# More modulation chunks on VectorE, shifted priorities, one-copy bank eviction, a new product order and a last norm with TensorE, in an encoder layer

## The chip, the cores and the metric

One core of a Trainium2 chip runs the whole kernel. The metric is the device time of one execution in microseconds (us), the median of several runs; lower is better. The engines are TensorE (PE in the profile; its weight loads have a row of their own, PEld), VectorE (DVE), ScalarE (ACT), GpSimd (POOL) and SyncE (SP), which issues most of the loads.

## The reference

One layer, 256 tokens of width 2048, fp32: attention and then an MLP, each with its own modulation from a vector c.

```python
# for each sub-layer:
h = x * (1 + scale(c)) + shift(c)
x = LayerNorm(alpha * x + (1 + gate(c)) * sublayer(h))
# attention: proj = h @ w_qkv + b_qkv, 32 query heads and 8 key/value heads of 64, rotary positions,
#   |q - k| <= 128, softmax with a learned sink per head, then o @ w_o + b_o
# MLP: relu(h @ w1 + b1)**2 @ w2 + b2, hidden width 8192
# LayerNorm: (x - mean) * rsqrt(var + 1e-5) * g + b over the 2048 columns
```

scale, shift and gate are matrix-vector products of the activated c with six matrices of 2048 x 2048.

## The kernel before

**Loads.** One stream (class `Stream`) holds a list of 1 MB loads, [128, 2048] fp32, planned once and issued in that order on SP's queue, as buffers (`raws`) come free. A load is either a part of a weight matrix, or a *modulation chunk*: two (for `m_gm`, one) groups of 128 rows of a modulation matrix. A group of matrices' columns (`Mod`) has 4 to 16 chunks; there are 80 of them beside the 16 of `m_gf`. `W1_FILL`, `SLOT_FILL` and `gf_fill` say how many late chunks stand between which weight loads.

**Modulation.** `Mod.step` uses a chunk in one of two ways. On TensorE, `quad` (L340) multiplies it in 32-column weight tiles with c and adds up in PSUM (8 instructions, 16 records of the trace each chunk). On VectorE, for the chunks whose number is in the tuple `dve`, it is multiplied by c's column, L376 (first) or L378 (added to the part so far), two of them for each chunk, and at the group's end one `quad` with ones sums over partitions. Then `columns` turns the row and `modulated(g)` (L565 to L567) scales and shifts x into a high part on ScalarE and a low part on VectorE.

**Weights.** Products of fp32 quality are made of three fp32r matmuls (`mm3`, L544 to L546): ScalarE rounds a load to its high part (`wh`, the cast L277), VectorE subtracts for the low part (`wl`, L230, *lows*). `Stream.pump` writes casts, lows and chunks into the program ahead of the matmuls that need them. Within an engine, the scheduler of the tile framework puts instructions in an order by priority (program order, if nothing shifts it) and readiness; on the chip each engine runs its list in that order.

**Stages.** qkv projection (to about 160 us) with the modulation groups 0 to 5; attention in 21 slots, where projection, rotary tables, scores, softmax, probabilities and the output projection are interleaved (to 355 us); the norm; the first block of W1 (L1032 to L1034); feed-forward blocks 1 to 3; the last columns of w2; the last norm.

**Feed-forward.** A block has 16 hidden tiles in 8 pairs. `hidden(f)` (L1060, L1062: 5.55 us) fills one PSUM bank with 256 columns of product and 256 of its correction, and `square_half` adds them and the bias, takes relu and square, and splits the result. `sides` makes sums of a pair's blocks (`sc`) for a scheme with 7 products instead of 8, and `chunk(i)` issues these 7 (21 matmuls) in two pieces around the second tile of the next pair:

```python
        for i in range(NP):
            g = chunk(i)
            if i + 1 < NP:
                hidden(2 * i + 2)
            next(g)
            if i + 1 < NP:
                hidden(2 * i + 3)
            for _ in g:
                pass
```

The products stay in seven PSUM banks over the whole block, so that one bank of the pool `psa` is left for the hidden tiles, and each must be read before the next tile starts.

**Tail.** For each half of the tokens (t = 0, 1), the last 512 columns of the output are multiplied, `add_gated` (L797 to L799) adds them to x and takes statistics, and the norm is written in four column blocks: L1217 (minus mean, times g) and L1222 (times rstd, plus b), one block of four with ScalarE (L1219) and GpSimd (L1220) instead.

## Time and profile before

| | |
|---|---|
| median of 3 runs | 1081.54 us (1081.45 to 1083.96) |
| the profiled execution | 1080.82 us, span 1079.0 us, mean TensorE clock 0.995 |
| instructions in the trace | 15651 |
| TensorE / its weight loads, busy | 97% / 79% |
| VectorE / ScalarE / GpSimd, busy | 86% / 57% / 3% |
| read from HBM | 289.57 MB |

The busy shares are means over the stages. Where TensorE is busy without a gap, a shorter wait elsewhere gives nothing; where it waits, the wait's last releaser counts. In rows of a timeline, the first number is the start, the second the duration, and the bracket the idle time before the row with what ended it.

### The profile page before, as it was taken

What the parts mean: (1) busy time and instruction counts of PE and PEld (TensorE: products, weight loads), DVE (VectorE), ACT (ScalarE), POOL (GpSimd) and SP (SyncE); (2) the same over time, 40 slices, a digit from 0 to 9 for tenths busy, and PEclk for the clock granted to TensorE, in tenths of its full rate; (3) what the DMA queues carried; (4) which work ended last, traced back from release to release, by engine and by line L of the source; (5) the groups of instructions that cost most, each with busy time, mean ns of one, the idle gap of its engine ahead of it and who ended that gap; (6) DMA issues with size and microseconds to landing.
All of it is one profiled execution on the core that took longest, in us unless ns stands there. A gap on an engine that the chain in (4) does not pass through costs nothing.

```text
span 1079.0 us, 15651 instructions
## 1 busy us (share of the span) xinstructions
PE 1049.8 (97%) x6018; PEld 847.9 (79%) x6018; DVE 926.3 (86%) x1371; ACT 611.4 (57%) x977; POOL 31.0 (3%) x56
## 2 busy tenths in 40 slices
PE   8889999999999999999999999999999999999995
PEld 6557677666667799988888888888888888888884
DVE  5598699988889898988679889969988887998997
ACT  5333347776773636644357677347767536776740
POOL 1000000001000000000000000000000001000001
PEclk9999999999999999999999999999999999999998
DMA  9999997779966798689725644954464684455632
GB/s 384 425 426 426 426 419 268 283 281 378 405 251 234 305 356 314 257 335 405 271 97 196 233 176 153 375 195 176 176 234 174 266 319 148 176 205 220 244 161 78
DMA packets 43371, 292.70 MB, mean 271 GB/s; under 512 B 5136, under 2 KB 5264, under 8 KB 9504
## 3 DMA queue, kind: packets, MB, share of 16 engines
q1 hardware_dynamic: 39312, 279.85, 66.7%
q0 software_dynamic: 3232, 10.50, 3.0%
q10 hardware_dynamic: 752, 1.35, 0.3%
q8 instruction: 47, 0.77, 0.3%
q14 instruction: 28, 0.23, 0.1%
HBM read 289.57 MB, written 2.11 MB: 270 GB/s over the span
## 4 chain that ended last, share of the span: by engine, by line
PE 85%; DMA 9%; DVE 4%; ACT 1%; issue 0%; SPq 0%; DVEq 0%; ACTq 0%
PE pa L1060 17%; PE pa L544 13%; PE pa L546 13%; PE pa L545 13%; PE pa L1062 8%; DMA raw<-in_wqkv 4%; PE pa L1033 3%; PE pa L1034 3%; PE pa L1032 3%; DMA raw<-in_modm 3%; PE pm L340 2%; DMA raw<-in_modf 2%; PE pa L733 1%; PE pa L789 1%; DVE wl L230 1%; DVE g L378 1%
## 5 line engine op out<-in xcount | busy, mean ns | idle before, releaser
L277 ACT CAST wh<-raw 128x1024 fp32r<-128x1024 f32 (+1 forms) x332 | 335.5, 1020 | 302.3 <-PE pa L546 136.2
L230 DVE TENSOR_TENSOR wl<-raw,wh 128x1024 fp32r<-128x1024 f32 (+1 forms) x332 | 388.5, 1183 | 79.8 <-ACT wh L277 74.6
L544 PE MATMUL pa<-wh,g 128*128 128x512 f32 x648 | 258.0, 399 | 4.4 <-ACT g L581 2.1
L546 PE MATMUL pa<-wh,g 128*128 128x512 f32 x648 | 252.2, 392 | 3.0 <-DVE g L567 2.4
L545 PE MATMUL pa<-wl,g 128*128 128x512 f32 x648 | 254.0, 392 | 0.0
L1060 PE MATMUL pa<-g,wh 128*128 128x512 f32 x768 | 193.4, 394 | 0.0
L1060 PEld LDWEIGHTS pa<-g,wh 128*128 128x128 f32 x768 | 139.8, 188 | 31.6 <-DVE rl L990 4.1
L544 PEld LDWEIGHTS pa<-wh,g 128*128 128x128 f32 x648 | 121.6, 188 | 39.3 <-issue 6.8
L546 PEld LDWEIGHTS pa<-wh,g 128*128 128x128 f32 x648 | 121.6, 188 | 33.1 <-DVE g L567 4.7
L545 PEld LDWEIGHTS pa<-wl,g 128*128 128x128 f32 x648 | 121.8, 188 | 25.9 <-issue 2.4
L1062 PEld LDWEIGHTS pa<-g,wl 128*128 128x128 f32 x768 | 104.8, 190 | 7.5
L1062 PE MATMUL pa<-g,wl 128*128 128x256 f32 x768 | 107.1, 283 | 0.0
L378 DVE SCALAR_TENSOR_TENSOR g<-raw,cact,g 128x1024 f32<-128x1024 f32 x65 | 82.6, 1278 | 1.5 <-DMA raw<-in_modf 1.3
L1033 PE MATMUL pa<-g,wh 128*128 128x256 f32 x256 | 72.7, 285 | 0.4 <-DVE g L961 0.4
L1032 PE MATMUL pa<-g,wh 128*128 128x256 f32 x256 | 72.6, 285 | 0.0
L1034 PE MATMUL pa<-g,wl 128*128 128x256 f32 x256 | 72.5, 284 | 0.0
L230 DVE TENSOR_TENSOR raw<-raw 128x1024 fp32r<-128x1024 f32 x48 | 58.7, 1223 | 8.5 <-ACT raw L277 6.6
L277 ACT CAST raw<-raw 128x1024 fp32r<-128x1024 f32 x48 | 50.6, 1054 | 12.0 <-PE pm L546 10.7
L340 PE MATMUL pm<-raw,cact 128*32 128x256 f32 (+2 forms) x768 | 47.3, 375 | 5.6 <-DMA raw<-in_modm 4.5
L1033 PEld LDWEIGHTS pa<-g,wh 128*128 128x128 f32 x256 | 49.1, 192 | 1.3 <-DVE g L961 0.8
L1032 PEld LDWEIGHTS pa<-g,wh 128*128 128x128 f32 x256 | 49.0, 192 | 0.4 <-ACT g L953 0.4
L1034 PEld LDWEIGHTS pa<-g,wl 128*128 128x128 f32 x256 | 49.1, 192 | 0.0
(220 smaller groups left out, 1210.0 us busy)
## 6 DMA issues: line engine op xcount, KB each, us to landing
raw<-in_w1b SPq DMA_DIRECT2D x48, 1024.0 KB, 5.6
raw<-in_w SPq DMA_DIRECT2D x40, 1024.0 KB, 8.4
raw<-in_modm SPq DMA_DIRECT2D x32, 1024.0 KB, 16.0
raw<-in_modf SPq DMA_DIRECT2D x32, 1024.0 KB, 8.8
raw<-in_wqkv SPq DMA_DIRECT2D x24, 1024.0 KB, 11.8
raw<-in_w2s SPq DMA_DIRECT2D x24, 1024.0 KB, 4.8
raw<-in_modgm SPq DMA_DIRECT2D x16, 1024.0 KB, 8.4
raw<-in_wo SPq DMA_DIRECT2D x16, 1024.0 KB, 7.6
```

What stands on the lines that cost most here:

```text
L230: self.pinned(nc.vector.tensor_sub(l[:, :w], r, f32(self.hs[n])[:, :w]))
L277: self.pinned(nc.scalar.copy(h[:, :s.shape[-1]], s))
L340: i = nc.tensor.matmul(self.ps[32 * j:32 * j + 32, :w], lhsT[j] if type(lhsT) is list else lhsT, rhs[j], start=self.first, stop=stop)
L378: nc.vector.scalar_tensor_tensor(p[:, :e], s, cact[:, kt:kt + 1], p[:, :e], op0=OP.mult, op1=OP.add)
L544: nc.tensor.matmul(ps, xh, wh, start=start, stop=False)
L545: nc.tensor.matmul(ps, xh, wl, start=False, stop=False)
L546: S.prev = nc.tensor.matmul(ps, xl, wh, start=False, stop=stop).ins
L1032: nc.tensor.matmul(o, wh(w, 128), hh, start=new, stop=False)
L1033: nc.tensor.matmul(o, wh(w, 128), hl, start=False, stop=False)
L1034: nc.tensor.matmul(o, wl(w, 128), hh, start=False, stop=end)
L1060: nc.tensor.matmul(ps, wh(k, 128), ff_in(k), start=k == 0, stop=False)
L1062: nc.tensor.matmul(ps[:, :256], wl(k, 128), ff_in(k)[:, :256], start=False, stop=k == NK - 1)
```

## The change

- **Chunks.** 40 chunks on VectorE instead of 36 (beside `m_gf`'s 16, unchanged), with other numbers in the tuples: one more in the fifth and one in the sixth group of the first modulation, one more in the second and one in the third group of the feed-forward's.
- **Load order.** New fill tables with the same totals. The first 56 loads on SP stay as they are; after these, chunks stand up to three places sooner or later between the weight loads.
- **Priorities.** `first(name)` wraps kinds of work in a priority shift, for the six names in `AHEAD` (evictions of partial sums, the sums of VectorE over w2's blocks, rotary products, the copies of transposed pairs and of probabilities, and `square_half`). Names that aren't in it are unchanged; `FREE = 9` leaves the pins of `modulated` as they were.
- **Bank.** `square_half` copies the hidden tile's whole bank with ScalarE, adds the halves in SBUF, and the bias goes into the relu.
- **Product order.** `chunk` yields after five of the seven products, and after two in the last two pairs of a block.
- **Tail.** For t = 0 all four column blocks are VectorE's. For t = 1, three of four blocks are scaled by g ahead of the statistics; TensorE adds b (a product with the identity) and -(mean/2)·q·g (one with a diagonal of it) in PSUM, and VectorE combines. `last_scalars` has fewer steps.

The fill tables and tuples as the diff has them:

```diff
+AHEAD = {'evict': -10, 'sums': -100, 'rope': 10, 'pairs': -10, 'probs': -100, 'square': -30}
+FREE = 9
...
+    def first(name):
+        n = AHEAD.get((stage[0], name), AHEAD.get(name))
+        return tc.high_priority(n) if n else nullcontext()
...
-    m_mix = groups(a["modm"], MIXG, [(), (), (), (0, 1, 4, 5), (1, 2, 4, 6, 7), (4, 7)])
-    m_ff = groups(a["modf"], FFG, [(0, 3, 7), (0, 1, 2, 4, 7), (3,), (0, 1, 2, 3, 4, 5, 6, 7)])
-    m_gm = Mod([a["modgm"][i] for i in range(NK)], 512, (3, 4, 5, 6, 9, 11, 12, 14), a["modgmb"])
+    m_mix = groups(a["modm"], MIXG, [(), (), (), (0, 1, 3, 6), (0, 2, 4, 5, 6, 7), (3, 5, 6)])
+    m_ff = groups(a["modf"], FFG, [(0, 3, 7), (0, 1, 3, 4, 5, 7), (3, 4), (0, 1, 2, 3, 4, 5, 6, 7)])
+    m_gm = Mod([a["modgm"][i] for i in range(NK)], 512, (3, 4, 5, 7, 9, 10, 12, 14), a["modgmb"])
...
-    SLOT_FILL = dict(enumerate([1, 1, 0, 1, 2, 2, 1, 1, 1, 3, 0, 3, 1, 5, 0, 4, 1, 4, 0, 2, 0, 0, 1], -2))
+    SLOT_FILL = dict(enumerate([0, 0, 3, 1, 2, 0, 0, 3, 0, 5, 1, 4, 1, 3, 0, 3, 2, 2, 0, 3, 0, 0, 1], -2))
...
     def square_half(ps, ft, u, uf, at):
 
         v = sml.tile([128, 512], F32, name="rl", tag="t2", bufs=4)
-        nc.scalar.activation(v[:, 256:], ps[:, 256:], AF.Identity, bias=b1[:, ft:ft + 1])
-        nc.vector.tensor_add(v[:, :256], v[:, 256:], ps[:, :256])
-        nc.scalar.activation(v[:, 256:], v[:, :256], AF.Relu)
...
+        with first("bank"):
+            nc.scalar.copy(v, ps)
+        with first("square"):
+            nc.vector.tensor_add(v[:, :256], v[:, :256], v[:, 256:])
+            nc.scalar.activation(v[:, 256:], v[:, :256], AF.Relu, bias=b1[:, ft:ft + 1])
...
             u = us[i]
+            at = 5 if i < NP - 2 else 2
+            for n, (p, x, c, r, e) in enumerate(((1, u, 0, 0, 0), (2, u, 2, 1, 1), (3, sc, 3, 1, 0),
+                                                 (5, sc, 0, 2, 0), (7, sc, 2, 2, 1))):
+                if n == at:
+                    yield
+                product(p, i, x, c, h[r], l[r], e)
+                if n in (0, 2, 4):
+                    S.done()
+            if at == 5:
+                yield
...
+        if t == 0:
+            add_gated(ps, t, 3, g2, st)
+            mv, rstd = norm_scalars(st[t])
+            for c in (1, 0, 2, 3):
+                z, (g, b) = part(xs, t, c), affine(c)
+                nc.vector.scalar_tensor_tensor(z, z, mv[:, 0:1], g, op0=OP.subtract, op1=OP.mult)
                 nc.vector.scalar_tensor_tensor(z, z, rstd, b, op0=OP.mult, op1=OP.add)
...
+            for c in range(3):
+                scaled(1, c)
+    pw = {}
+    for c in (1, 2, 3):
+        pw[c] = psa.tile([128, 512], F32, name="pa")
+        g, b = affine(c)
+        tc.keep_in_program_order(nc.tensor.matmul(pw[c], ident, b, start=True, stop=False))
+    with tc.high_priority(200):
+        add_gated(ps, 1, 3, g2, st)
+        rstd, nm = last_scalars(st[1])
+        dg = sml.tile([128, 128], F32, name="dg", tag="t2", bufs=4)
+        nc.scalar.activation(dg, ident, AF.Copy, scale=nm)
+    scaled(1, 3)
+    g, b = affine(0)
+    w = sml.tile([128, 512], F32, name="w", tag="t2", bufs=4)
+    nc.vector.scalar_tensor_tensor(w, g, nm, b, op0=OP.mult, op1=OP.add)
+    for c in range(4):
+        z, (g, b) = part(xs, 1, c), affine(c)
+        if c:
+            nc.tensor.matmul(pw[c], dg, g, start=False, stop=True)
+        nc.vector.scalar_tensor_tensor(z, z, rstd, pw[c] if c else w, op0=OP.mult, op1=OP.add)
+        store(1, c, z)
```

(`scaled(t, c)` multiplies a block by -g/2, `store` issues its write to HBM.) Line numbers of the changed kernel are 9 to 83 higher for the same work: L230 is L239, L376 and L378 are L389 and L391, L566 and L567 are L582 and L583, L1060 and L1062 are L1095 and L1097, L277 is L288, L544 to L546 are L558 to L560, and L797 to L799 are L826 to L828. Three places show how instructions move.

VectorE around the modulation of x for the fifth group (x in g4_595, its scales in scm; wl are lows, and g4_1092 or g4_1050 is VectorE's part of the sixth group's modulation). Before:

```order
L417 TENSOR_SCALAR scm_113<-scm_113 128x4
L230 TENSOR_TENSOR wl_1090<-raw_935,wh_1066 128x1024
L230 TENSOR_TENSOR wl_1161<-raw_935,wh_1088 128x1024
L376 TENSOR_SCALAR g4_1092<-raw_953,cact_110 128x1024
L566 TENSOR_SCALAR g4_595<-g4_595,scm_113,shm_114 128x256
L378 SCALAR_TENSOR_TENSOR g4_1092<-raw_953,cact_110,g4_1092 128x1024
L567 TENSOR_TENSOR g4_1114<-g4_595,g4_1113 128x256
L566 TENSOR_SCALAR g4_595<-g4_595,scm_113,shm_114 128x256
L567 TENSOR_TENSOR g4_1114<-g4_595,g4_1113 128x256
```

After:

```order
L431 TENSOR_SCALAR scm_113<-scm_113 128x4
L389 TENSOR_SCALAR g4_1050<-raw_899,cact_110 128x1024
L391 SCALAR_TENSOR_TENSOR g4_1050<-raw_899,cact_110,g4_1050 128x1024
L239 TENSOR_TENSOR wl_1079<-raw_929,wh_1055 128x1024
L239 TENSOR_TENSOR wl_1149<-raw_929,wh_1077 128x1024
L582 TENSOR_SCALAR g4_595<-g4_595,scm_113,shm_114 128x256
L583 TENSOR_TENSOR g4_1102<-g4_595,g4_1101 128x256
```

The chunk of the sixth group's modulation (L376 and L378, now L389 and L391) has moved from between the two lows and L567 to a place ahead of the lows.

PE in a feed-forward block, from a hidden tile's last correction (L1062, now L1097) to the next tile's first product; pa, pt and pm are PSUM banks, sc, g4 and raw the hidden values and the weights. Before, the shorter of the two gaps of a pair:

```order
L1062 MATMUL pa_5685<-g4_4137,wl_5643 128x256 x2
L544 MATMUL pt_5428<-wh_5641,g4_5533 128x512
L545 MATMUL pt_5428<-wl_5662,g4_5533 128x512
L546 MATMUL pt_5428<-wh_5641,g4_5533 128x512
L544 MATMUL pa_5429<-wh_5660,g4_5533 128x512
L545 MATMUL pa_5429<-wl_5673,g4_5533 128x512
L546 MATMUL pa_5429<-wh_5660,g4_5533 128x512
L544 MATMUL pa_5430<-wh_5660,sc_5675 128x512
L545 MATMUL pa_5430<-wl_5673,sc_5675 128x512
L546 MATMUL pa_5430<-wh_5660,sc_5675 128x512
L544 MATMUL pt_5431<-raw_5671,sc_5675 128x512
L1060 MATMUL pa_5754<-g4_3396,wh_5723 128x512 x2
```

After, the shorter gap:

```order
L1097 MATMUL pa_5586<-g4_4112,wl_5572 128x256 x2
L1097 MATMUL pa_5586<-g4_4113,wl_5572 128x256 x2
L558 MATMUL pa_5405<-raw_5526,sc_5497 128x512
L559 MATMUL pa_5405<-raw_5526,sc_5497 128x512
L560 MATMUL pa_5405<-raw_5526,sc_5497 128x512
L558 MATMUL pa_5406<-raw_5526,g4_5350 128x512
L559 MATMUL pa_5406<-raw_5526,g4_5350 128x512
L560 MATMUL pa_5406<-raw_5526,g4_5350 128x512
L1095 MATMUL pa_5657<-g4_3372,wh_5570 128x512 x2
```

The gap between two hidden tiles had 10 matmuls here and 11 at the other tile of the pair; now it has 6 here and 15 there.

ScalarE around the eviction of a hidden tile (pa to rl) in such a pair. Before:

```order
L277 CAST wh_5738<-raw_5602 128x1024
L1008 CAST sc_5675<-sf_5676 128x512
L277 CAST wh_5748<-raw_5645 128x1024
L989 ACTIVATE rl_5728<-pa_5685,pack_87 128x256
L277 CAST wh_5771<-raw_5645 128x1024
L277 CAST wh_5791<-raw_5726 128x512
L991 ACTIVATE rl_5728<-rl_5728 128x256
```

After:

```order
L288 CAST wh_5625<-raw_5548 128x1024
L288 CAST raw_5643<-raw_5548 128x1024
L288 CAST wh_5695<-raw_5574 128x1024
L1022 COPY rl_5629<-pa_5586 128x512
L1025 ACTIVATE rl_5629<-rl_5629,pack_87 128x256
L1027 ACTIVATE uf_5506<-rl_5629 128x256
L288 CAST raw_5676<-raw_5548 128x1024
L1029 CAST g4_5505<-uf_5506 128x256
```

The bank copy L1022 takes the place of L989; relu L1025 and square L1027 follow it with no cast between, and there is again a cast of the next weights ahead of the copy.

VectorE in the tail. Before, from `add_gated` of t = 1 on:

```order
L797 TENSOR_TENSOR tmp<-pa,g4b 128x512
L798 TENSOR_TENSOR g_2474<-g_2474,tmp 128x512
L799 BN_STATS st_9555<-g_2474 128x6
L803 BN_AGGR mv<-st_9555 128x2
L805 TENSOR_SCALAR ve<-mv 128x1
L1217 SCALAR_TENSOR_TENSOR g_2470<-g_2470,mv,g_9546 128x512
L809 RECIPROCAL r_9876<-sd 128x1
L1217 SCALAR_TENSOR_TENSOR g_2468<-g_2468,mv,g_9546 128x512
L811 SCALAR_TENSOR_TENSOR qq<-r_9876,ve 128x1
L1217 SCALAR_TENSOR_TENSOR g_2472<-g_2472,mv,g_9547 128x512
L812 TENSOR_SCALAR qq<-qq 128x1
L1217 SCALAR_TENSOR_TENSOR g_2474<-g_2474,mv,g_9547 128x512
```

After, first what stands ahead of t = 0's chain:

```order
L239 TENSOR_TENSOR g_9701<-raw,g_9699 128x1024
L239 TENSOR_TENSOR g_9705<-raw,g_9703 128x1024
L239 TENSOR_TENSOR g4b<-raw,g4b 128x1024 x2
L1271 SCALAR_TENSOR_TENSOR g_2466<-g_2466,g_9522 128x512
L1271 SCALAR_TENSOR_TENSOR g_2468<-g_2468,g_9522 128x512
L1271 SCALAR_TENSOR_TENSOR g_2470<-g_2470,g_9523 128x512
L826 TENSOR_TENSOR tmp<-pa,g4b 128x512
L827 TENSOR_TENSOR g_2472<-g_2472,tmp 128x512
L828 BN_STATS st_9530<-g_2472 128x6
L832 BN_AGGR mv<-st_9530 128x2
```

Then, from `add_gated` of t = 1 on:

```order
L826 TENSOR_TENSOR tmp<-pa,g4b 128x512
L827 TENSOR_TENSOR g_2472<-g_2472,tmp 128x512
L828 BN_STATS st_9531<-g_2472 128x6
L1248 BN_AGGR mv<-st_9531 128x2
L1271 SCALAR_TENSOR_TENSOR g_2472<-g_2472,g_9523 128x512
L1252 TENSOR_SCALAR ve<-mv 128x1
L1254 RECIPROCAL r_9860<-sd 128x1
L1256 SCALAR_TENSOR_TENSOR qq<-r_9860,ve 128x1
L1257 SCALAR_TENSOR_TENSOR qq<-qq,r_9860 128x1
L1259 SCALAR_TENSOR_TENSOR nmr<-mv,qq 128x1
L1300 SCALAR_TENSOR_TENSOR w<-g_9522,nmr,g_9524 128x512
L1305 SCALAR_TENSOR_TENSOR g_2466<-g_2466,qq,w 128x512
```

Three of the four scalings by g (L1271) have moved ahead of t = 0's `add_gated`; of t = 1's norm, one is left behind the aggregate, and the last four steps read PSUM or w.

More of the change, by code (lines that the diff above doesn't have):

```diff
@@ L229, in low @@
                 l = (g4, g4b)[kept - 1](F32R) if kept > 0 else wlp.tile([128, 1024], F32R, name="wl")
-            self.pinned(nc.vector.tensor_sub(l[:, :w], r, f32(self.hs[n])[:, :w]))
+            with first("low"):
+                self.pinned(nc.vector.tensor_sub(l[:, :w], r, f32(self.hs[n])[:, :w]))
             self.ls.append(l)
@@ L276, in pump @@
                     s = raw[:, j * 1024:j * 1024 + 1024]
-                self.pinned(nc.scalar.copy(h[:, :s.shape[-1]], s))
+                with first("cast"):
+                    self.pinned(nc.scalar.copy(h[:, :s.shape[-1]], s))
                 self.hs.append(h)
@@ L564, in modulated @@
             xt, sc, sh = xts.pop(k0 + k), scm[:, k0 + k:k0 + k + 1], shm[:, k0 + k:k0 + k + 1]
[L565 to L567 removed]
+            with first("modulated"):
+                keep(nc.scalar.activation(hh[:, s], xt, AF.Identity, scale=sc, bias=sh))
+                keep(nc.vector.tensor_scalar(xt, xt, sc, sh, op0=OP.mult, op1=OP.add))
+                keep(nc.vector.tensor_sub(hl[:, s], xt, f32(hh[:, s])))
         held[g] = hh, hl
@@ L579, in evict @@
             if new:
-                bq(pss[t], c)
-                nc.scalar.copy(av, pss[t])
-            else:
-                nc.vector.tensor_add(av, av, pss[t])
+                with first("evict0"):
+                    bq(pss[t], c)
+                    nc.scalar.copy(av, pss[t])
+            else:
+                with first("evict"):
+                    nc.vector.tensor_add(av, av, pss[t])
     def banks():
@@ L713, in pairs_T @@
                     nc.tensor.transpose(pt[:, i * 256 + t * 128:i * 256 + t * 128 + 128], src[:, x:x + 128], ident)
-            nc.scalar.copy(out[:, pr * 512:pr * 512 + 512], pt)
+            with first("pairs"):
+                nc.scalar.copy(out[:, pr * 512:pr * 512 + 512], pt)
         return out
@@ L742, in scores @@
[L742 to L750 removed]
+                with first("scores"):
+                    nc.tensor.matmul(pss[s][:, i], qT[j][p, x:x + 128], kT[p, j * 256:j * 256 + 256],
+                                     start=True, stop=True)
@@ L879, in hybrid_kernel @@
     S.behind = True
+    stage[0] = "attention"
     for n in range(21):
@@ L935, in hybrid_kernel @@
     S.behind = False
+    stage[0] = "feed"
     ff_columns(0)
```

249 lines of the change are left out of this document (132 added, 117 removed).

## The prediction

> **What bounds the kernel now.** I read the page first: engine shares, slices, chain.
>
> ```profile
> span 1079.0 us, 15651 instructions
> PE 1049.8 (97%) x6018; PEld 847.9 (79%) x6018; DVE 926.3 (86%) x1371; ACT 611.4 (57%) x977; POOL 31.0 (3%) x56
> PEclk9999999999999999999999999999999999999998
> DMA  9999997779966798689725644954464684455632
> PE 85%; DMA 9%; DVE 4%; ACT 1%; issue 0%; SPq 0%; DVEq 0%; ACTq 0%
> ```
>
> TensorE (PE) is busy for 97% of the span at full clock and holds 85% of the chain. So the time can change in three ways only: work taken off PE, the some 29 us in which PE isn't busy, and the end after its last matmul. The waits view says what PE waited for in the middle:
>
> ```profile
> PEld pa L1060 <- DVE rl L990: 4.1, 11, 0.4
> PE pa L546 <- DVE g L567: 2.4, 2, 1.7
> PE pm L340 <- DMA raw<-in_modf: 1.1, 1, 1.1
> PE pm L340 <- DVE g L378: 0.8, 1, 0.8
> PE pa L546 <- DVE g L792: 0.6, 1, 0.6
> ```
>
> These five are 9.0 us. The other side of the change is VectorE (DVE), which gets more to do. Its load by stage, from the windows view (columns: window, length, busy PE, PEld, DVE, ACT, POOL, clock, DMA share, GB/s):
>
> ```profile
> 100.00:150.00 50.00, 48.28 (x298) 34.04 (x297) 37.88 (x56) 19.64 (x25) 1.90 (x2) 1.00 1.01 426
> 150.00:200.00 50.00, 50.00 (x262) 36.36 (x261) 48.76 (x89) 32.08 (x74) 0.48 (x1) 1.00 0.75 286
> 250.00:300.00 50.00, 48.61 (x321) 32.00 (x321) 41.23 (x88) 32.30 (x82) 3.40 (x5) 1.00 1.00 406
> 350.00:400.00 50.00, 48.49 (x417) 43.35 (x416) 45.26 (x78) 28.26 (x40) 0.00 (x0) 1.00 0.85 318
> ```
>
> VectorE has 12 us free of 50 in the projection, but only 1 to 9 in the windows after it. DMA is full in the projection (1.01) and again at 250 to 300 us.
>
> **A. The projection: −2.2 us.** One stall is worth a close look, the 1.7 of the second wait row:
>
> ```profile
> 112.56 3.66 PE L340 MATMUL pm<-raw,cact 128*32 128x256 f32 x64
> 114.14 2.36 DVE L230 TENSOR_TENSOR wl<-raw,wh 128x1024 fp32r<-128x1024 f32 x2 [3.44 <-ACT wh L277]
> 116.42 0.74 DVE L376 TENSOR_SCALAR g<-raw,cact 128x1024 f32<-128x1024 f32 x1
> 116.95 0.40 PE L545 MATMUL pa<-wl,g 128*128 128x512 f32 x1
> 117.41 1.28 DVE L378 SCALAR_TENSOR_TENSOR g<-raw,cact,g 128x1024 f32<-128x1024 f32 x1
> 118.60 0.41 DVE L567 TENSOR_TENSOR g<-g,g 128x256 fp32r<-128x256 f32 x1
> 119.07 0.50 PE L546 MATMUL pa<-wh,g 128*128 128x512 f32 x1 [1.72 <-DVE g L567]
> ```
>
> A modulation chunk (L376 and L378, 2.02 us) stands on VectorE between the lows L230 and the L567 that PE waits for. Before those lows VectorE had been idle for 3.44 us. In the changed order the chunk stands ahead of the lows, so its 2.02 us fall into that idle time, and L567 can end right after the lows. PE would go on some 0.23 us after the L545 at 116.95, which saves 1.7 to 1.8 us. The load it reads is an earlier one than that of the lows, so it should have landed; if not, the lows wait behind it, and the 2 us are lost again.
>
> Two chunks more leave PE in this stage. One costs 3.66/4 = 0.92 us of PE (64 matmul records are four chunks), and 2.0 to 2.6 us of VectorE. The one of the fifth group lies where PE waits for loads anyway (DMA share 1.01): nothing. The one of the sixth counts 0.9. I give 0.5 back, for the modulated inputs of the sixth group come later behind the extra chunk, and SP's loads in this stage can't go faster than 426 GB/s. Sum −1.8 − 0.9 + 0.5 = −2.2; ends −3 and 0.
>
> **B. Norm and first feed-forward stage: −1.4 us.**
>
> ```profile
> 353.78 1.22 DVE L230 TENSOR_TENSOR wl<-raw,wh 128x1024 fp32r<-128x1024 f32 x1
> 354.54 0.39 PE L546 MATMUL pa<-wh,g 128*128 128x512 f32 x1
> 355.51 0.68 DVE L797 TENSOR_TENSOR tmp<-pa,g4b 128x512 f32<-128x512 f32 x1
> 360.83 0.44 PE L947 MATMUL pt<-ident,g 128*128 128x128 f32 x2
> ```
>
> After the last matmul of the attention output (ended 354.93) the chain to the next stage runs over VectorE; its first step L797 came 0.58 us late, behind L230. In the new order that low stands behind it: −0.5. PE fills this stretch with modulation chunks, so the chunk that the second feed-forward group hands to VectorE saves nothing here. The one of the third group lies among W1's products, where PE is the limit: −0.9. Ends −2 and +0.5 (VectorE is 45.26 of 50 there).
>
> **C. Attention: 0, from −2 to +4.** Four chunks are about 10 us more for VectorE in all, at most half of them in its busy windows. The three short stalls that PE has there by the waits rows (1.1, 0.8, 0.6) can go with the smoother spread of loads, and others can come: a chunk half of 1.28 us that stands ahead of what PE needs costs up to that each. Three of those would be 4 us. The priorities shift evictions, rope sums and copies by a few places; no row prices that alone. I take nothing.
>
> **D. Feed-forward: −3.0 us.** In each pair of hidden tiles PE waits for a bank:
>
> ```profile
> 612.44 1.04 ACT L277 CAST wh<-raw 128x1024 fp32r<-128x1024 f32 x1
> 613.39 0.47 ACT L989 ACTIVATE rl<-pa,pack 128x256 f32<-128x256 f32 x1
> 613.52 1.22 DVE L230 TENSOR_TENSOR wl<-raw,wh 128x1024 fp32r<-128x1024 f32 x1 [0.26 <-ACT wh L277]
> 614.66 0.41 DVE L990 TENSOR_TENSOR rl<-rl,pa 128x256 f32<-128x256 f32 x1
> 614.79 0.39 PE L544 MATMUL pt<-raw,sc 128*128 128x512 f32 x1
> 615.13 2.14 PE L1060 MATMUL pa<-g,wh 128*128 128x512 f32 x8
> 1024.31 0.59 ACT L1117 COPY w<-pa 128x512 f32<-128x512 f32 x1
> ```
>
> The bank is read twice, by ScalarE (L989) and then by VectorE (L990), and L990 stood behind a low of 1.22 us. It ended at 615.07, and PE took the bank at 615.13, 0.11 later than its pace allowed for PE itself and 0.37 for its weight load. Now ScalarE copies the whole bank; the copy of that size in L1117 took 0.59, and VectorE's queue no longer counts. The new order of the products leaves 15 matmuls after the first tile of a pair (15 × 0.227 = 3.4 us), but only 6 after the second (1.36 us; before, 10 and 11). A cast of 1.04 us stands ahead of the copy. If it begins 0.8 us before the tile ends, as its wh buffer comes free, it ends 0.25 after it, the copy at 0.84, and with 0.06 for the hand-over PE has the bank at 0.90, 0.46 before it needs it. So the stalls go: 4.1 us. But the weight load overlaps PE, so I count three quarters: −3.0. In the chain that turns a tile into u and sc (u is needed 5.55 + 1.36 = 6.9 us after the second tile, before 8.0), L995 and L1008 stood behind two or three casts; in the new order fewer stand between. Ends −4.5 and 0.
>
> The Trainium skill (Perfetto Trace Analysis, section Optimizing Scalar/DVE Operations) speaks against this edit: where Scalar and Vector aren't saturated but cause bubbles elsewhere, it says, breaking instructions up may let work end sooner, and here two halves become one whole. By that rule D would be zero, as in the third rival below. The rows speak for the whole: 0.59 in one against 0.47 + 0.41 with 0.8 of waiting between two queues.
>
> **E. The tail: −1.0 us.**
>
> ```profile
> 1066.27 0.39 PE L546 MATMUL pa<-g4b,g 128*128 128x512 f32 x1
> 1066.70 0.69 DVE L797 TENSOR_TENSOR tmp<-pa,g4b 128x512 f32<-128x512 f32 x1 [1.46 <-PE pa L546]
> 1068.88 0.26 DVE L803 BATCH_NORM_AGGREGATE mv<-st 128x2 f32<-128x24 f32 x1
> 1072.34 3.08 DVE L1222 SCALAR_TENSOR_TENSOR g<-g,r,g 128x512 f32<-128x512 f32 x3
> 209.44 1.94 PE L789 MATMUL pa<-g,g 128*64 128x512 f32 x8
> 1069.00:1071.00 2.00, 0.00 (x0) 0.00 (x0) 1.97 (x7) 0.20 (x1) 0.00 (x0) 1.00 0.00 0
> 1071.00:1073.00 2.00, 0.00 (x0) 0.00 (x0) 1.96 (x5) 0.67 (x1) 0.00 (x0) 0.52 0.00 0
> ```
>
> Before, VectorE ends at 1072.34 + 3.08 = 1075.42. After, up to the aggregate at 1069.14 all is the same: the three steps for the last rows that move up stand ahead of the first half's chain, in PE's time, and the step that the first half takes back from ScalarE and GpSimd fits the 1.46 us of idle time. Then come one step of 0.74, five small ones of 0.15 to 0.2 (to 1070.7), and the step w and four last ones of 0.74 at a pace of 0.72: 1070.7 + 5 × 0.72 = 1074.3. PE's products of diag(nm) with g are fp32, some 0.48 us each by L789 (four in 1.94); begun at 1071.1 the last ends at 1072.6, ahead of the VectorE step that reads it (1073.6). That is −1.1, I take −1.0.
>
> The clock matters little. It was full in the window up to 1071 and 0.52 in the next, so it fell some 4.4 us after PE's end at 1066.66. The new products with ident keep PE busy until about 1068.1, so the idle time before the diag products is 3 us. If the clock falls all the same, they take 2.9 us, to 1074.0, and the last step slips by 0.4. The Trainium skill (TensorE: Matmul & The Clock Gate, What's actually happening) gives a free-running window of some 3.4 us; by it the clock is still full here, or at worst halved, as in these two sums. Ends −1.3 and +0.5 (a queue or semaphore that I don't see).
>
> **The sum.** −2.2 − 1.4 + 0 − 3.0 − 1.0 = −7.6 us. The profiled execution took 1080.82 (span 1079.0 and 1.8 around it), so 1073.2 for its like; it is 0.7 below the median of 1081.54, so 1073.9 for a median.
>
> **Rivals.**
> - *ScalarE's copy comes too late* (slower). If a cast has just begun when the second tile ends, the bank is free after 1.04 + 0.59 + 0.06 = 1.69 us, and with a second small step ahead at 1.86 and more, where PE has 1.36. Eighteen pairs (six in each of three blocks) would stall 0.5 each: +9, and D's 3 is gone: 1073.9 + 12 = 1085.9. It decides when the release comes later than 1.36 us after the tile. For it: ScalarE's casts are queued ahead, 1.04 each; against: it is idle for 43% of the span, and casts wait for buffers that PE frees at known points. 0.13.
> - *VectorE becomes the bound in attention and W1* (no change). C at its end of +4, and B at +0.5: −7.6 + 4 + 1.9 = −1.7, 1079.8. For it: 48.76 of 50 busy at 150 to 200. Against: the new tables spread loads more evenly. 0.14.
> - *The order gives nothing, only PE's chunks do*: D at 0, A at −1, the rest as forecast: −3.4, 1078.1. The copy's gain would be hidden, since PE's own matmuls can catch up. 0.14.
> - *All named stalls go*, in attention too: −7.6 − 2.5 − 1.2: 1070.2. 0.12.
> - *The forecast*: 1073.9, 0.45. Left over for mixed mishaps: 0.02.
>
> About 0.3% (3.2 us) is what a measurement of this kernel can tell from no change. Faster by more (under 1078.3): the forecast, all stalls gone, about two thirds of the third rival and a little of the second, 0.69. Slower by more: the first rival and the leftovers, 0.15. Within: 0.16. The range reaches from 1069 (all stalls gone, with something more) to 1083 (the second rival and the lesser half of the first).
>
> **What would show it.** Right: no wait at the second hidden tile's bank; the bank copy ends within 1.3 us of each tile; the stall near 117 us gone; the last VectorE step at about 1.1 us less after PE's last product of us; PE busy about 3 us less. Wrong: a waits row of PE's weights on the bank copy, with 18 entries of 0.5; new PE waits on L378's successor between 150 and 400 us; a clock of half in the diag products; lows that wait for a chunk's load near 112 us.

## The result, and the profile after

The changed kernel takes 1074.96 us (median of 4 runs, 1072.99 to 1075.15) against 1081.69 for the kernel before; the ratio is 0.9935, 95% interval 0.9923 to 0.9946. That is 6.7 us less, where the prediction had 7.6 (1073.9). The profiled execution, 1072.99 us, was the fastest of the four.

From the page of the changed kernel, the busy time of the engines and the chain that ended last:

```profile
span 1070.9 us, 15564 instructions
PE 1049.5 (98%) x5966; PEld 850.2 (79%) x5966; DVE 936.2 (87%) x1382; ACT 620.1 (58%) x976; POOL 27.5 (3%) x54
PE 86%; DMA 7%; DVE 5%; issue 1%; ACT 1%; DVEq 0%; ACTq 0%; SPq 0%
```

VectorE has 10 us more to do, as it should (8 chunk halves of 1.28). TensorE's busy time seems unchanged, but 5.6 us of it are new: the six records each of L1291 and L1304 in the tail (2.73 + 2.84). So elsewhere it is 5.9 us less. The waits view, first of TensorE and then of its weight loads:

```profile
PE pm L352 <- DMA raw<-in_modm: 5.0, 4, 2.4
PE pa L1304 <- ACT dg L1296: 1.7, 1, 1.7
PE pa L560 <- DVE g L583: 1.7, 2, 1.5
PE pt L979 <- DVE g L857: 0.8, 1, 0.8
PE pa L1068 <- DVE g L993: 0.8, 1, 0.8
PE pa L559 <- DVE wl L239: 0.7, 2, 0.4
```

The eleven waits of weight loads on the hidden tile's bank, the wait on the chunk L378 and the one on in_modf are gone. What is left of L560's wait is almost all another one, 1.5 us at 78 us. New are waits at the norm (L979, L1068) and on lows (L559).

To see where the time went, the table takes the stages from the traces: to the first scores; to the start of the last product of the attention output; to the first product of W1; to the last of W1; its w2 to the first tile of block 1 (87.4 to 87.7 in all); the blocks to the end of the last w2 product; from there to the end of the span. In us, one execution each. The experiments e1 to e12 below are in it too.

| kernel | projection | attention | norm | W1 | blocks | tail |
|---|---|---|---|---|---|---|
| before | 165.7 | 188.8 | 8.6 | 97.2 | 519.0 | 12.4 |
| changed | 163.9 | 183.9 | 7.8 | 99.2 | 517.4 | 11.4 |
| e1 changed again | 164.2 | 184.5 | 7.7 | 99.3 | 518.3 | 13.0 |
| e2 no shifts | 164.1 | 184.9 | 7.8 | 98.9 | 519.1 | 11.4 |
| e3 old chunks and tables | 167.4 | 194.5 | 11.1 | 96.7 | 516.2 | 11.4 |
| e4 old eviction and order | 164.1 | 183.9 | 7.7 | 98.6 | 518.9 | 11.4 |
| e5 as e3, no shifts | 166.1 | 187.9 | 8.7 | 97.2 | 518.6 | 11.4 |
| e6 new chunks and tables only | 165.0 | 183.9 | 7.9 | 99.8 | 522.4 | 12.4 |
| e7 old tables, new chunks | 164.8 | 190.6 | 11.1 | 98.0 | 516.1 | 12.8 |
| e8 old tail | 163.9 | 184.3 | 7.8 | 99.2 | 517.0 | 12.4 |
| e9 old SLOT_FILL | 164.7 | 190.1 | 8.0 | 99.9 | 517.5 | 11.4 |
| e10 as e3, no shift of probs | 165.7 | 189.7 | 8.6 | 97.2 | 516.2 | 11.4 |
| e11 old eviction, new order | 163.9 | 184.1 | 7.8 | 99.8 | 531.6 | 11.4 |
| e12 gf spread | 165.3 | 184.2 | 7.7 | 99.8 | 516.1 | 11.4 |

So the change is −1.8 in the projection, −4.9 in attention, −0.8 in the norm, +2.0 in W1, −1.6 in the blocks, −1.0 in the tail: −8.1 between the two profiled executions.

In the blocks, the timeline of the changed kernel shows what replaced the bank's wait (second tile of a pair, its 6 products, the next tile):

```profile
615.00 1.12 PE L1097 MATMUL pa<-g,wl 128*128 128x256 f32 x8
615.21 1.05 ACT L288 CAST wh<-raw 128x1024 fp32r<-128x1024 f32 x1 [0.80 <-PE pa L1095]
616.16 0.58 ACT L1022 COPY rl<-pa 128x512 f32<-128x512 f32 x1
617.35 0.39 PE L1095 MATMUL pa<-g,wh 128*128 128x512 f32 x1
```

The tile ends at 616.12. The cast ahead of the copy began 0.91 us earlier, and the copy is done 0.62 us after the tile. The next tile begins 1.23 us after it and finds the bank free for 0.6 us.

### The profile page after: what moved, and what is told of

It is laid out like the page before. It is cut to its first block, busy times and chain, and to the rows that moved or that the text cites. A ratio compares the mean times of both kernels' runs of the same rounds, so it can differ in the third digit from the quotient of the medians.

```text
span 1070.9 us, 15564 instructions
## 1 busy us (share of the span) xinstructions
PE 1049.5 (98%) x5966; PEld 850.2 (79%) x5966; DVE 936.2 (87%) x1382; ACT 620.1 (58%) x976; POOL 27.5 (3%) x54
## 4 chain that ended last, share of the span: by engine, by line
PE 86%; DMA 7%; DVE 5%; issue 1%; ACT 1%; DVEq 0%; ACTq 0%; SPq 0%
PE pa L1095 16%; PE pa L558 13%; PE pa L560 13%; PE pa L559 13%; PE pa L1097 9%; DMA raw<-in_modm 5%; PE pa L1068 3%; PE pa L1069 3%; PE pa L1067 3%; PE pm L352 3%; PE pa L756 2%; DVE wl L239 2%; PE pa L817 1%; PE pt L800 1%; DMA raw<-in_w 1%
## 5 line engine op out<-in xcount | busy, mean ns | idle before, releaser
L288 ACT CAST wh<-raw 128x1024 fp32r<-128x1024 f32 (+1 forms) x332 | 336.2, 1021 | 272.0 <-PE pa L560 133.5
L239 DVE TENSOR_TENSOR wl<-raw,wh 128x1024 fp32r<-128x1024 f32 (+1 forms) x332 | 388.1, 1181 | 77.3 <-ACT wh L288 71.9
L558 PE MATMUL pa<-wh,g 128*128 128x512 f32 x648 | 257.6, 399 | 2.7 <-ACT g L598 1.7
L559 PE MATMUL pa<-wl,g 128*128 128x512 f32 x648 | 254.1, 392 | 0.8 <-DVE wl L239 0.7
L560 PE MATMUL pa<-wh,g 128*128 128x512 f32 x648 | 252.6, 392 | 1.7 <-DVE g L583 1.7
L1095 PE MATMUL pa<-g,wh 128*128 128x512 f32 x768 | 191.3, 391 | 0.0
L1095 PEld LDWEIGHTS pa<-g,wh 128*128 128x128 f32 x768 | 140.7, 188 | 27.9 <-issue 0.8
L558 PEld LDWEIGHTS pa<-wh,g 128*128 128x128 f32 x648 | 121.8, 188 | 39.6 <-issue 6.4
L560 PEld LDWEIGHTS pa<-wh,g 128*128 128x128 f32 x648 | 121.7, 188 | 31.2 <-DVE g L583 3.9
L559 PEld LDWEIGHTS pa<-wl,g 128*128 128x128 f32 x648 | 121.9, 188 | 27.0 <-DVE wl L239 2.1
L1097 PEld LDWEIGHTS pa<-g,wl 128*128 128x128 f32 x768 | 104.8, 190 | 7.5
L1097 PE MATMUL pa<-g,wl 128*128 128x256 f32 x768 | 107.1, 282 | 0.0
L391 DVE SCALAR_TENSOR_TENSOR g<-raw,cact,g 128x1024 f32<-128x1024 f32 x73 | 92.8, 1279 | 1.2 <-DMA raw<-in_modf 0.8
L1068 PE MATMUL pa<-g,wh 128*128 128x256 f32 x256 | 73.4, 287 | 0.8 <-DVE g L993 0.8
L239 DVE TENSOR_TENSOR raw<-raw 128x1024 fp32r<-128x1024 f32 x48 | 58.3, 1220 | 0.6 <-ACT raw L288 0.6
L288 ACT CAST raw<-raw 128x1024 fp32r<-128x1024 f32 x48 | 49.8, 1043 | 2.8 <-DVE raw L250 1.4
L1068 PEld LDWEIGHTS pa<-g,wh 128*128 128x128 f32 x256 | 49.8, 194 | 1.3 <-DVE g L993 1.3
L352 PE MATMUL pm<-raw,cact 128*32 128x256 f32 (+2 forms) x704 | 43.4, 378 | 5.0 <-DMA raw<-in_modm 5.0
```

The source lines that it names most:

```text
L239: self.pinned(nc.vector.tensor_sub(l[:, :w], r, f32(self.hs[n])[:, :w]))
L288: self.pinned(nc.scalar.copy(h[:, :s.shape[-1]], s))
L352: i = nc.tensor.matmul(self.ps[32 * j:32 * j + 32, :w], lhsT[j] if type(lhsT) is list else lhsT, rhs[j], start=self.first, stop=stop)
L391: nc.vector.scalar_tensor_tensor(p[:, :e], s, cact[:, kt:kt + 1], p[:, :e], op0=OP.mult, op1=OP.add)
L558: nc.tensor.matmul(ps, xh, wh, start=start, stop=False)
L559: nc.tensor.matmul(ps, xh, wl, start=False, stop=False)
```

## The experiments

Four questions: which part makes the gain in attention, what the priority shifts do, which half of the block's edit matters, and what the tail is worth. Ratios are to the kernel before, run beside each.

**e1, the changed kernel again.** 

> The changed kernel itself once more, as the measure for the three runs beside it. Expected: 1075.0 us within 1, about 6.7 us under the kernel before.

Measured 1073.83 us (1073.62 to 1076.12), ratio 0.9933 [0.9919, 0.9948]. The median is 1.2 us under the first one, but the kernel before was lower too (1081.23), and the ratio is the same. Its stages agree with the first profile within 0.9, but for the tail: VectorE ended 7.9 us after the last w2 product in both, and the last writes took 1.6 us longer.

**e2, no priority shifts.**

```diff
-AHEAD = {'evict': -10, 'sums': -100, 'rope': 10, 'pairs': -10, 'probs': -100, 'square': -30}
+AHEAD = {}
```

> The changed kernel with an empty table of priority shifts. The attention stage became 4.9 us shorter, where the prediction had zero. Theory 1 (the prediction's: the priorities give nothing by themselves, the gain there comes from where chunks and loads now stand): within 1 us of the changed kernel. Theory 2 (the priorities set that gain, above all evictions and copies of probabilities that no longer stand ahead of what TensorE waits for): 3 to 5 us slower than the changed kernel, most of it between the first scores and the last product of the attention output.

Measured 1076.73 us, ratio 0.9961 [0.9947, 0.9975], 2.9 us more than e1. Neither theory: attention keeps its gain (184.9 us), so the shifts don't make it; the blocks are 0.8 to 1.7 us longer, which is where the table shows most of the loss. There TensorE's weight loads wait for the sums `sc`: 3.3 us in 8 waits for the step L1044 and 2.5 in 7 for L1043, against 1.2 and 0.6 in 3 each in the changed kernel. The shifts are worth about 3 us here.

**e3, old chunks and old tables.** The tuples of `m_mix`, `m_ff`, `m_gm` and the lists `W1_FILL`, `SLOT_FILL`, `gf_fill` as before the change:

```diff
-    m_mix = groups(a["modm"], MIXG, [(), (), (), (0, 1, 3, 6), (0, 2, 4, 5, 6, 7), (3, 5, 6)])
+    m_mix = groups(a["modm"], MIXG, [(), (), (), (0, 1, 4, 5), (1, 2, 4, 6, 7), (4, 7)])
...
```

> The changed kernel with the old tuples of chunks and the old three fill tables; all else as changed. Theory 1: slower by A, B and what attention gained, 1.8 + 3.7 = 5.5 us, and the stall of 1.7 to 1.9 us near 117 us is back. Theory 2 (priorities made the gain in attention): slower by only 1.8 us in the projection and by some 2 us for two chunks of TensorE work, so 2 to 4 us.

Measured 1084.94 us, ratio 1.0032 [1.0021, 1.0042]: 11.1 us slower than e1, and slower than the kernel before, though bank copy, order, shifts and tail were all in it. Both theories expected far less. The timeline of its ScalarE in attention shows the largest piece:

```profile
191.75 2.02 ACT L288 CAST wh<-raw 128x1024 fp32r<-128x1024 f32 x2
193.64 1.74 ACT L788 ACTIVATE g<-g,rs 128x256 f32<-128x256 f32 x4
195.25 1.09 ACT L803 COPY g<-pt 128x512 f32<-128x512 f32 x2
```

And its waits view:

```profile
PE pa L817 <- ACT g L803: 3.5, 1, 3.5
```

The two copies of probabilities (L803) stand behind two casts and four normalisations (L788), and TensorE's products with the values wait 3.5 us for them. After that the clock falls too (windows; the last figures of a row are clock, DMA share and GB/s):

```profile
190.00:194.00 4.00, 2.38 (x14) 1.76 (x14) 3.78 (x8) 4.00 (x12) 0.00 (x0) 1.00 0.69 250
194.00:198.00 4.00, 2.10 (x6) 0.76 (x8) 3.83 (x4) 2.34 (x6) 0.00 (x0) 0.63 0.68 238
198.00:202.00 4.00, 4.00 (x13) 1.63 (x10) 0.38 (x1) 0.58 (x1) 0.00 (x0) 0.52 0.85 301
```

A mean of 0.63 and 0.52 over 4 us each is 2 × (0.37 + 0.48) × 4 = 6.8 us at half clock. TensorE was busy for 6.0 us of these (2.1 in the second window and 3.9 after it), so it lost about 3.0 us of work, nearly as much again as the wait itself.

**e4, old eviction and old product order.** `square_half` and `chunk` as before the change; shifts, tables and tail as changed.

> The changed kernel with the old eviction of a hidden tile in two halves and the old order of the seven products. Theory 1 (the bank's release through VectorE's queue was the stall): 1.5 to 3 us slower than the changed kernel, with waits of TensorE's weight loads on the step of VectorE that frees the bank (about ten of 0.4 us). Rival (that stall was hidden, the blocks' 1.5 us came from the other order of casts and sums by the priorities): within 0.7 us of the changed kernel.

Measured 1075.57 us, ratio 0.9952 [0.9938, 0.9966], 1.7 us more than e1 beside it, and the waits are back, 13 of them:

```profile
PEld pa L1094 <- DVE rl L1023: 3.1, 13, 0.3
```

Theory 1, at its low end. The intervals of e1 and e4 overlap, so the size is loose; the wait's return isn't.

**e5, old chunks and tables, no shifts.** e3 with `AHEAD = {}`.

> The changed kernel with the old tuples and fill tables and no priority shifts: what is left of the change is the bank copy, the product order and the tail. With the old tables the shifted kernel was 11 us slower than the changed one, with a wait of 3.5 us of TensorE for ScalarE's copy of probabilities. Theory 3 (the shifts suit only the new tables: on the old ones they cost): about 1081.2 - 1.7 (bank and order) - 1.0 (tail) = 1078.5 us, and that wait is gone. Rival (the tables are worth 11 us by themselves): 1084 us or more, slower than the kernel before.

Measured 1080.15 us, ratio 0.9988 [0.9979, 0.9998]. Theory 3: on the old tables the same shifts that gain 2.9 us on the new ones cost 4.8 us (0.9988 against 1.0032). The value is 1.6 us over what the sum gave; bank copy, order and tail together are worth 1.3 us here, not 2.7. The table says why: without the shifts, the blocks gain only 0.4 us (518.6), with them 2.8 (516.2 in e3), and the tail its 1.0. The wait of 3.5 us for the copies of probabilities is gone, as expected, and the waits for `sc` in the blocks are those of e2.

**e6, the new chunks and tables alone**, in the kernel before.

> The kernel before with the new tuples and fill tables alone. Theory 3 (shifts and tables gain only together): 1074.0 + 2.9 (shifts) + 1.7 (bank and order) + 1.0 (tail) = 1079.6 us, 1.6 us under the kernel before. The prediction's steps A and B by themselves: 3.6 us under it, 1077.6. Rival (tables worth 11 us by themselves): 1070 to 1073.

Measured 1080.02 us, ratio 0.998 [0.9969, 0.9991]: theory 3. The table tells more than the total: attention has its whole gain (183.9 us), but W1 is 2.6 and the blocks 3.4 us longer than before. In the blocks, TensorE waits for lows with the new `gf_fill`, and still for the bank (weight loads):

```profile
PEld pa L1060 <- DVE rl L990: 4.5, 12, 0.4
PEld pa L545 <- DVE wl L230: 3.1, 3, 1.5
```

**e7, old tables, new chunks.** Only the three lists go back; TensorE's share of the work is that of the changed kernel.

> The changed kernel with the old three fill tables, but the new tuples, so that TensorE keeps the same work and only the loads' places among each other go back. If the places of the loads make the gain in attention (chunks arrive when VectorE and DMA have room): 4 to 9 us slower than the changed kernel, with waits on in_modf again. If the number of chunks on VectorE makes it: within 2 us of it.

Measured 1081.37 us, ratio 0.9996 [0.9985, 1.0007], 6.6 us more than the changed kernel (0.9935), and TensorE waits on in_modf again:

```profile
PE pm L352 <- DMA raw<-in_modf: 2.7, 2, 1.4
```

One of the two waits (1.3) is in attention, the other in the norm, where the kernel before had its own of 1.1 us. So the four chunks taken off TensorE don't make the gain without the places of the loads. They aren't worth nothing: e7 is 3.9 us under e3, from which it differs by the tuples alone, and the wait for probabilities of 3.5 us in e3 is not among e7's long ones.

**e8, old tail.**

> The changed kernel with the old last norm (both halves on VectorE with ScalarE and GpSimd). By the prediction's step E: 1.0 us slower than the changed kernel, between the last product of w2 and the end, 12.3 us there against 11.3. Rival (TensorE's products at 0.9 us each, twice what the prediction took, eat the gain): within 0.3 us of it.

Measured 1075.15 us, ratio 0.9944 [0.9927, 0.9961]; the stage is 12.4 us against 11.4, as expected. By the ratios it is 1.0 us, inside the intervals. The rival's price was right (in the changed kernel a product with the diagonal takes 0.95 us), but it did not eat the gain.

**e9, old SLOT_FILL alone.**

```diff
-    SLOT_FILL = dict(enumerate([0, 0, 3, 1, 2, 0, 0, 3, 0, 5, 1, 4, 1, 3, 0, 3, 2, 2, 0, 3, 0, 0, 1], -2))
+    SLOT_FILL = dict(enumerate([1, 1, 0, 1, 2, 2, 1, 1, 1, 3, 0, 3, 1, 5, 0, 4, 1, 4, 0, 2, 0, 0, 1], -2))
```

> The changed kernel with the old SLOT_FILL alone, the table that sets which chunks stand between the weight loads of the 21 attention slots; W1_FILL and gf_fill stay new. If this table makes the gain in attention: the stage from the first scores to the last product of the attention output lasts about 190 us as with all three old tables (184 in the changed kernel), and the kernel takes 4 to 7 us more than the changed one. If the other two tables make it: within 1.5 us of it.

Measured 1080.24 us, ratio 0.9987 [0.9978, 0.9997], 5.6 us more than the changed kernel (0.9935), and attention lasts 190.1 us. With the new chunks, this one list holds the gain; the new list with the old chunks was not run. The windows view over just that stage, of e9 and then of the changed kernel:

```profile
164.70:354.80 190.10, 188.13 (x1055) 129.14 (x1056) 173.06 (x340) 123.06 (x298) 9.01 (x14) 1.00 0.77 293
```

```profile
163.90:347.80 183.90, 183.73 (x1055) 128.40 (x1055) 170.57 (x338) 123.50 (x298) 9.03 (x14) 1.00 0.79 302
```

The records are the same, 1055 of TensorE. Its idle time is 2.0 us in e9 and 0.2 in the changed kernel; the other 4.4 us lie inside its busy time. Most of them are in the products that use half of TensorE's array: the scores (L756, weights on 64 rows) and the values (L817, weights on 64 columns). The same windows for L756 alone, then for L817, each time e9 first:

```profile
164.70:354.80 190.10, 20.01 (x128) 11.91 (x128) 1.00 0.77 293
163.90:347.80 183.90, 18.15 (x128) 11.01 (x128) 1.00 0.79 302
```

```profile
164.70:354.80 190.10, 16.78 (x64) 3.97 (x64) 1.00 0.77 293
163.90:347.80 183.90, 15.50 (x64) 3.88 (x64) 1.00 0.79 302
```

That is 1.9 + 1.3 = 3.1 us more for the same records. Where two such products, one for each half, stand next to each other in TensorE's list, they run side by side; in e9 some of them are apart. A group of eight records of scores, in the changed kernel and then in e9:

```profile
170.39 1.13 PE L756 MATMUL pa<-g,g 64*128 64x256 f32 x8
```

```profile
171.15 1.96 PE L756 MATMUL pa<-g,g 64*128 64x256 f32 x8
```

In the first the records start in twos, in the second one after the other. One group of values in e9 is parted by the closing sum of a modulation group (L352), which stands in its middle at 312 us. So the places of the loads also change the order of TensorE's own list. The scheduler's reason for each place, and the remaining 1.3 us, stay open.

**e10, old chunks and tables, all shifts but that of probs.**

```diff
-AHEAD = {'evict': -10, 'sums': -100, 'rope': 10, 'pairs': -10, 'probs': -100, 'square': -30}
+AHEAD = {'evict': -10, 'sums': -100, 'rope': 10, 'pairs': -10, 'square': -30}
```

> The changed kernel with old tuples and tables, and the shift of the copies of probabilities taken out, the other five kept. With all shifts it took 3.5 us more than the kernel before, without any 1.3 us less, and TensorE once waited 3.5 us for that copy, which stood behind two casts and four normalisations on ScalarE. If that copy's place is the whole cost: 1080.2 us (3 to 5 us less than with all shifts), and the wait is gone. If the other shifts (sums of w2's blocks, evictions, rotary products) cost as much: 1083 us or more.

Measured 1078.66 us, ratio 0.9978 [0.9969, 0.9987], 5.8 us less than e3. One entry was the whole cost. The other five seem to gain 1.1 us even on the old tables (against e5), but the two intervals overlap: the blocks are 2.4 us shorter than in e5, attention is 1.8 us longer. The wait for the copies was not gone, but 1.0 us instead of 3.5 (waits), and the clock stayed full (windows):

```profile
PE pa L817 <- ACT g L803: 1.0, 1, 1.0
```

```profile
194.00:198.00 4.00, 4.00 (x25) 3.10 (x22) 3.28 (x10) 1.93 (x5) 0.00 (x0) 1.00 0.54 229
```

**e11, old eviction, new product order.** `square_half` as before, `chunk` as changed.

> The changed kernel with the old eviction in two halves, and the new order of products (15 and 6 between tiles). The kernel before freed a bank some 2.2 us after its tile's end; with 6 matmuls TensorE has 1.36 us. If that path is what stalled, TensorE now waits about 0.8 us after each second tile, 18 times: 10 to 15 us slower than the changed kernel, with waits of that number. If the two edits are independent: 0.5 to 1 us slower.

Measured 1088.59 us, ratio 1.0069 [1.0055, 1.0082], 14.5 us more than the changed kernel by the ratios (0.0134 × 1081.7): the first case, though with 14 waits where 18 were expected. One second tile of it in the timeline:

```profile
617.78 1.12 PE L1096 MATMUL pa<-g,wl 128*128 128x256 f32 x8
618.93 0.48 ACT L1022 ACTIVATE rl<-pa,pack 128x256 f32<-128x256 f32 x1
619.35 1.22 DVE L239 TENSOR_TENSOR wl<-raw,wh 128x1024 fp32r<-128x1024 f32 x1
620.49 0.41 DVE L1023 TENSOR_TENSOR rl<-rl,pa 128x256 f32<-128x256 f32 x1
620.96 1.68 PEld L1094 LDWEIGHTS pa<-g,wh 128*128 128x128 f32 x8 [0.65 <-DVE rl L1023]
```

And its waits of weight loads:

```profile
PEld pa L1094 <- DVE rl L1023: 8.6, 14, 1.1
PEld pa L560 <- DVE sc L1043: 4.3, 14, 0.4
```

The bank came free 2.0 us after the tile, behind a low, and sc came late as well. With the old order the same eviction cost 1.7 us (e4, with that order). So with the old eviction the new order costs. What the copy gives with the old order was not run, so the two parts' shares of the 1.7 us are not known.

**e12, gf's last chunks spread over two blocks.**

```diff
-    gf_fill = [2, 1, 0, 0, 0, 0, 3, 0, 1, 0, 1, 0, 1, 0, 2, 0, 0, 0, 2, 0, 0, 0, 1, 2, 0, 0, 0, 0, 0, 0, 0, 0]
+    gf_fill = [2, 1, 0, 0, 0, 0, 3, 0, 1, 0, 1, 0, 1, 0, 2, 0, 0, 0, 1, 0, 0, 0, 0, 1, 0, 0, 0, 1, 0, 1, 1, 0]
```

> The changed kernel with the last five chunks of gf spread over the first two instead of the first of the feed-forward blocks' w2 loads (as before the change, but for their number). In the changed kernel TensorE waits 0.4 to 1.0 us at 681 and 0.6 at 707 us for lows that came late there. If the chunks beside those loads make them late: 1 to 1.6 us faster than the changed kernel, about 0.992 of the kernel before, and no such waits. If the waits only move to the second block: no change.

Measured 1073.04 us (1072.39 to 1073.83), ratio 0.9926 [0.9913, 0.9938], the lowest median of the study. The blocks fell to 516.1 us, 1.3 to 2.2 less than in the two profiles of the changed kernel, and no wait of TensorE on lows is left there. The total is 0.8 us better by the ratios, but the intervals overlap: the stage shows it, the whole time doesn't prove it.

## Why the prediction was right, and where it wasn't

The total came out (7.6 forecast, 6.7 measured by medians, 8.1 between the profiled executions), but as a sum of terms that missed in both directions.

- **A, projection, −2.2.** Measured −1.8. The stall at 117 us is gone for the reason given: the chunk runs ahead of the lows, and L560 follows L559 without a wait (changed kernel):

```profile
111.30 0.75 DVE L389 TENSOR_SCALAR g<-raw,cact 128x1024 f32<-128x1024 f32 x1
114.23 2.36 DVE L239 TENSOR_TENSOR wl<-raw,wh 128x1024 fp32r<-128x1024 f32 x2 [0.86 <-ACT wh L288]
117.56 0.40 PE L560 MATMUL pa<-wh,g 128*128 128x512 f32 x1
```

  Earlier in the stage other waits moved: TensorE's wait for L583 at 78 us grew from 0.7 to 1.5, and one of 1.9 at 75 us is gone. The prediction counted only the stall at 117 us.
- **B, norm and W1, −1.4.** Measured −0.8 + 2.0 = +1.2. The norm's chain is shorter as forecast. Two sentences fail. One is that the third group's chunk "lies among W1's products", −0.9: TensorE multiplies no chunk there in either kernel (8 records each, a closing sum). By the records of L340 and L352, two of the four chunks left the projection (512 to 480), one attention (224 to 208) and one the norm (88 to 72), so this term belonged to C. The other is that the second feed-forward group's chunk "saves nothing here": it cost. In the norm TensorE now has 72 records of chunks to fill that stretch instead of 88, is idle more, and the clock falls (changed kernel, then before):

```profile
350.00:354.00 4.00, 2.91 (x50) 1.41 (x42) 3.93 (x24) 1.84 (x4) 0.00 (x0) 1.00 1.02 410
354.00:358.00 4.00, 2.41 (x12) 1.51 (x12) 3.93 (x8) 4.00 (x9) 0.00 (x0) 0.99 1.01 422
358.00:362.00 4.00, 4.00 (x21) 3.88 (x21) 3.83 (x11) 4.00 (x7) 0.00 (x0) 0.58 0.95 401
```

```profile
359.00:363.00 4.00, 3.15 (x32) 1.53 (x32) 2.95 (x15) 2.24 (x5) 0.00 (x0) 1.00 1.01 426
363.00:367.00 4.00, 3.60 (x25) 2.81 (x23) 3.23 (x12) 4.00 (x9) 0.00 (x0) 1.00 1.01 426
```

  2 × 0.42 × 4 = 3.4 us at half clock, 1.7 us of work, most of the +2.0; the wait of L1068, 0.8 us where the same product waited 0.4 before, is the rest. In its one profiled execution every kernel with the new tuples has the fall, and of those with the old ones only e3, which lost TensorE 2.1 us on a load there. It was not tried to keep TensorE fuller there, so that the missing chunk is the cause is argued from this pattern, not shown by an experiment of its own.
- **C, attention, 0 from −2 to +4.** Measured −4.9, outside its own ends. The prediction named three stalls and took the rest of TensorE's time there as work. One of the three, the 1.1 for in_modf, is not in attention but in the norm, at 359 us. Against the kernel before, about 1.4 of the 4.9 us is idle time (1.6 to 0.2), 1.3 the chunk that left TensorE there, and 1.8 scores and values that run side by side more often (18.84 to 18.15 and 16.57 to 15.50 us busy). The last of these is in no sentence of the prediction. The new chunks and tables alone give it (18.11 and 15.50 in e6), and without the new SLOT_FILL it is lost (e9). This is the term that carried the result, and since the forecast had zero here, that the total came out is in part luck. Of the rival in which only TensorE's chunks give something, e7 and e9 leave little: with the same four chunks off TensorE, but the loads or those of the attention slots alone in their old places, the kernel is at 0.9996 and 0.9987 of the time before.
- **The priorities, 0.** The step that failed is to take them as a term of its own, worth nothing: they are worth −2.9 us on the new tables (e2) and +4.8 on the old ones (e3 against e5), all of the latter from one entry (e10). No single number was there to be forecast.
- **D, blocks, −3.0.** Measured −1.6 in the profile, 1.7 by e4. The mechanism was right: cast 0.91 us ahead of the tile's end (0.8 forecast), bank free after 0.62 (0.90), 0.6 us to spare (0.46). The sentence that fewer casts stand ahead of u and sc holds only with the shifts: without them (e2, e5) the waits for the bank are nearly gone too (0.4 to 0.7 us), but those for sc are 5.8 us instead of 1.8, and the blocks are 518.6 to 519.1 us. What was missed is on the other side of the sum: gf's chunks beside the w2 loads of block 1 made the casts late (ScalarE idle for a load) and with them lows that TensorE waits for. By the order of the loads in the traces, the last two of these chunks stand 28 and 30 weight loads earlier than in the kernel before, not up to three as the text on the change has it.

```profile
679.40 2.00 ACT L288 CAST wh<-raw 128x1024 fp32r<-128x1024 f32 x2 [5.67 <-DMA raw<-in_w]
680.48 2.36 DVE L239 TENSOR_TENSOR wl<-raw,wh 128x1024 fp32r<-128x1024 f32 x2 [0.98 <-ACT wh L288]
681.76 0.50 PE L559 MATMUL pa<-wl,g 128*128 128x512 f32 x1 [0.27 <-DVE wl L239]
```

  e12 took these waits away and the blocks came to 516.1 us, 2.9 under the kernel before, the forecast's size; e3, e7 and e10, which have the shifts (e10 all but one), the copy and the order with the old `gf_fill`, have 516.1 to 516.2 too.
- **E, tail, −1.0.** Measured −1.0, with one price wrong: a product with the diagonal took 0.95 us (six records in 2.84 for three), not 0.48: L789, from which the price was taken, runs two products side by side. The last VectorE step waited for it a little, and the norm's small steps were quicker than forecast.

```profile
1059.20 0.39 PE L560 MATMUL pa<-g4b,g 128*128 128x512 f32 x1
1059.43 2.73 PE L1291 MATMUL pa<-g,ident 128*128 128x512 f32 x6
1063.87 2.84 PE L1304 MATMUL pa<-g,dg 128*128 128x512 f32 x6 [1.71 <-ACT dg L1296]
1065.04 2.46 DVE L1305 SCALAR_TENSOR_TENSOR g<-g,qq,pa 128x512 f32<-128x512 f32 x3
```

- **The slower rival** did not happen in the changed kernel, and e11 shows by another path what a late bank costs: with the eviction that passes through VectorE, six matmuls are too few, and the price was 14.5 us, near the rival's +12. The second rival's mechanism, a busy VectorE, was not seen in the changed kernel's attention, where TensorE is idle for 0.2 us. The advice of the Trainium skill (Perfetto Trace Analysis, Optimizing Scalar/DVE Operations) that breaking instructions up may let work end sooner doesn't help here: one copy of 0.58 us frees the bank after 0.62 us, two halves on two engines after 2.0.

## What to carry to other kernels

Where one stream feeds everything, the places of the loads among each other can be worth more than the work that they bring: 5.6 us from one list of 23 numbers (e9), where four chunks taken off the bounding engine are 3.7 us of its work. Part of this need not show as a wait: products that can run side by side did so or not by their order, so compare the busy time of the same records too. Tables of priorities and of load places are tuned to each other, so test them together, and read a part's worth from both sides (with and without the rest). Work of the bounding engine that fills a wait is not free to remove, since the idle time may cost clock afterwards.

## What the runs showed of the hardware

- After a stretch of 8 us in which TensorE was busy for 2.91 and 2.41 of 4 us, its clock was halved for 3.4 us, with TensorE fully busy by then. The longest single gaps in that stretch were about 0.8 us (the waits of L979 and L1068). The same stretch in the kernel before, with 3.15 and 3.60 of 4 in the windows shown, kept full clock. In the same place e12 has a clock of 0.91 over 345 to 385 us, which is 7.2 us at half, the changed kernel 0.96, 3.2 us:

```profile
345.00:385.00 40.00, 37.38 (x303) 33.51 (x302) 35.35 (x70) 22.55 (x34) 0.00 (x0) 0.91 0.81 310
```

```profile
345.00:385.00 40.00, 37.31 (x316) 33.43 (x315) 35.80 (x68) 24.10 (x36) 0.00 (x0) 0.96 0.86 323
```

  So the loss comes in pieces of about 3.4 us, one or two of them. The Trainium skill (TensorE: Matmul & The Clock Gate, What's actually happening) has a free-running window of 3.4 us, and the traces agree with its length. Part of the 2 us spread between runs of one kernel may come from this; that was only argued.
- An fp32 product with weights 128 wide took two records of 0.46 to 0.47 us (L1291, L1304), at full clock, while eight records of L789 with weights 64 wide took 1.94 us in all. That is because two products with weights 64 wide run side by side. In e9 four records (two products) took as long as two (one product) elsewhere:

```profile
190.57 1.08 PE L817 MATMUL pa<-g,g 128*64 128x512 f32 x4 [0.31 <-ACT g L803]
310.99 1.07 PE L817 MATMUL pa<-g,g 128*64 128x512 f32 x2
```
